# A hybrid decoder block on one core: bias masks moved into the recurrence, indexer loads brought forward, convolution columns moved behind the softmax, softmax division moved to the end

## The chip, the cores and the metric

The kernel runs on one core of a Trainium2 chip. A core has TensorE (PE, matrix products; its weight loads are listed as PEld), VectorE (DVE), ScalarE (ACT), GpSimd (POOL) and SyncE (SP, which here only issues DMAs). Matrix products end in PSUM; everything else works from SBUF, and DMAs move data to and from device memory. The metric is the device time of one execution in microseconds, lower is better.

## What is computed

One layer of a decoder block over 512 tokens of width 1024, all in float32. The part that the change touches:

```
h = adaLN(RMSNorm(x), c)              # c gives shifts, scales and gates ("modulation")
z = h @ w_in                          # columns: attention | RWKV | convolution | 3 gates
o_attn = dsa_attention(z_attn, positions, rel_bias)
o_rwkv = rwkv7_mix(z_rwkv, ...)       # a recurrence over the tokens, 8 heads of 64
o_conv = c_b * causal_dwconv(c_c * c_x)
merged = sum(sigmoid(z_gate_i) * (o_i @ w_branch[i]))
x = x + g1 * (merged @ w_o);  then a ConvGLU feed-forward with its own adaLN; final RMSNorm

# dsa_attention, per query block of 128:
score = sum_h relu(qi_h . ki) * wi_h          # "indexer", 8 heads
keep the 128 best keys of each query
logits = q . k / 8 + rel_bias[bucket(pos_q - pos_k)]    # 32 buckets
o = softmax(logits over the kept keys) @ v
```

## The kernel before

The program is written as a sequence of tile operations. A planner lays it down as one fixed stream per engine: among the instructions whose inputs and buffers it expects to be ready, it takes the one that stands first in the program. `tc.high_priority(offset=n)` moves a block ahead by n places in that ranking (a negative n moves it back), and `tc.issue_after(ins)` keeps a block's instructions behind `ins` on the engine of `ins`. The engines then run their streams in order and wait on semaphores.

**Columns.** `z_col` computes 128 columns of `h @ w_in`, transposed: 8 blocks of 128 rows, three matmuls of 512 columns each (lines 177 to 179), since every float is split into a high and a low part (the split of the weights is at lines 163 on ScalarE and 165 on GpSimd, three buffers each). These column matmuls have no dependence on the attention or the recurrence, so they fill TensorE wherever the chains leave room. The order in the program is: RWKV columns and their chunk preparation; the inversion of a triangular 32x32 system on VectorE (the loop with lines 569 and 571); a DMA round trip for its result (`Dm`); the recurrence in 8 steps (lines 608 to 648); its norm (lines 656 to 675); 12 convolution columns with `conv3`; the attention columns (4 of the indexer's queries, one for its keys and weights, 4 of q, 4 of k, then v); the indexer and top-k; the softmax; then three branches (RWKV, convolution, attention), each with 8 gate columns and 8 branch products.

**Attention columns** are written to device memory as a high and a low part (`split_out`, lines 752 to 755) and loaded again by head: `load_q` and its neighbours issue these loads on GpSimd's queue. The indexer's query and key loads (`qi`, `ki`) stand behind the v columns.

**Bias.** For each key block b, and for 32 groups of 4 keys, VectorE writes a mask tile (line 721: position of the query minus key position at least the threshold of the bucket, 128 rows for 4 keys x 32 buckets, up to 512 queries wide); TensorE multiplies each 128-query block of a mask with the bias differences `dmat` (line 727, two matmuls of 32 columns, high and low part). ScalarE scales the result into `stage` (line 733), and a DMA writes it to `bias_d`. One step is 16 masks; the 8 steps run between the attention columns of q and k. `thr`, the thresholds, come from four loads of the positions early on.

**Indexer and top-k.** 24 pairs of matmuls (`two_pass`, lines 800 and 801), relu on ScalarE, weighted sums on VectorE (832, 834), then 16 rounds of "8 largest" and "replace" for each of three query blocks (839, 840).

**Softmax.** For 4 pairs of heads and 4 query blocks: the bias block is loaded (`bt`), the selection mask is added on GpSimd (867); `two_pass` gives the logits; VectorE adds the bias and takes the row maximum (874) and negates it (876); ScalarE takes the exponential with row sums (878); VectorE takes reciprocals (879) and multiplies each row (881); TensorE transposes the 128x128 blocks (885); ScalarE copies them into `pT` (889). When all four query blocks of a pair are there, 8 matmuls of up to 512 columns give the output, transposed (894), and ScalarE copies it to `o_at` (897).

**Modulation.** `ada_parts` loads 256 KB pieces of `ada_w` and sums them on VectorE (215, 217); one such step is issued with `next(ada)`: four in the k columns, four for each gate column. `finish` ends each group of 8 with TensorE (202) and VectorE (203).

**Memory.** Tiles live in pools that grow from the left or right end of SBUF; a pool opened after another was closed on the same side takes its space, and waits, tile by tile, for its last users. The bias pool `bi` was on the right, where `att` and `ix` (the indexer's operands) come after it. `wk` is a ring of four 512-wide work tiles.

Of the kernel before, what the change touches and what calls it, by code (L numbers as in the profile page):

```python
# [10 lines left out]
F32 = mybir.dt.float32  # L11
# [48 lines left out]
def hybrid_block(ctx, tc, ins, out, consts, dbg=None, stop=99):  # L60
# [286 lines left out]
    def rel_pos(name, shape, aps, pos0, pool, keep=None):  # L347

        pi, lo_i = (T(name + x, shape, I32, pool=pool) for x in "il")
        for dst, ap in aps:  # L350
            SP.dma_start(dst(pi), ap)
        DVE.tensor_scalar(lo_i, pi, 0xFFFF, None, op0=ALU.bitwise_and)
        DVE.tensor_scalar(pi, pi, 16, None, op0=ALU.arith_shift_right)
        rel = T(name, shape, pool=keep or pool)
# [3 lines left out]
        return rel  # L358

    def bias_operands():  # L360
# [7 lines left out]
        thr = rel_pos("thr", [128, 4, 32], [  # L368
            ((lambda t, b=b: t[:, b, :]), dram("positions", b * 128, [[0, 32], [32, 4], [1, 32]])) for b in range(4)], pos0, start.pool, sb)
        DVE.tensor_scalar(thr, thr, kc[:, K_THR:K_THR + 1], None, op0=ALU.add)  # L370
# [25 lines left out]
        return pos0, thr, pw, dmat  # L396

    with tc.issue_after(h_last):
        pos0, thr, pw, dmat = bias_operands()
# [155 lines left out]
    ep.close()  # L555

# [9 lines left out]
    for s_ in range(31):  # L566
# [4 lines left out]
        DVE.tensor_tensor(Ts[:, s_ + 1:, :w], Ts[:, s_ + 1:, :w], t_, op=ALU.add)  # L571
# [28 lines left out]

    S_ = None
    for c in range(8):
        if c:
# [80 lines left out]
    cvp = left_pool("cvp")  # L684
    o_cv = T("o_cv", [128, 4, 512], pool=cvp.pool)

# [6 lines left out]
    for m in range(4):  # L693
        ps_c = z_col(C_CONV + 512 + m * 128)
        cc = wk()
        ACT.activation(cc, ps_c, AF.Copy)
        ps_x = z_col(C_CONV + 1024 + m * 128)
        DVE.tensor_tensor(cc, cc, ps_x, op=ALU.mult)
        cy = wk()
        conv3(cy, cc, cw[:, m, :])  # L700
        ps_b = z_col(C_CONV + m * 128)
        DVE.tensor_tensor(o_cv[:, m, :], cy, ps_b, op=ALU.mult)  # L702
    tap("o_conv", o_cv)


    adp = left_pool("adp")
    bi = right_pool("bi")

    posq = rel_pos("posq", [128, S], [(lambda t: t, dram("positions", 0, [[0, 128], [1, S]]))], pos0, bi.pool)
    bias_d = tc.dram_tile([4, 128, H, 4, 128], F32, name="bias_d")  # L710

    def bias_steps():
        for b in range(4):
            n = S - 128 * b
            stage = {}
            for half in range(2):
                mk = []
                for g in range(16):
                    gg = half * 16 + g
                    m_ = T("mk", [128, 512], F16, tag="mk", bufs=18, pool=bi.pool)  # L720
                    DVE.tensor_scalar(m_[:, :n], posq[:, b * 128:], thr[:, b, gg:gg + 1], None, op0=ALU.is_ge)  # L721
                    mk.append(m_)
                for qb in range(b, 4):
                    ps = sd_bank()
                    for g in range(16):
                        for i in range(2):
                            PE.matmul(ps[:, g * 32:(g + 1) * 32], mk[g][:, (qb - b) * 128:(qb - b + 1) * 128],  # L727
                                      dmat[:, i].rearrange("p j h -> p (j h)"), start=(i == 0), stop=(i == 1))
                    if half == 0:
                        stage[qb] = T("stage", [128, 8, 4, 2, 16], tag="stage", bufs=4, pool=bi.pool)  # L730
                    src = ps.rearrange("p (g j h) -> p h j g", g=16, j=4)
                    for hh in range(2):
                        ACT.activation(stage[qb][:, hh * 4:hh * 4 + 4, :, half, :], src[:, hh * 4:hh * 4 + 4], AF.Copy,
                                       scale=pw[:, 0:1])
                    if half == 1:
                        ACT.dma_start(bias_d[qb, :, :, b, :], stage[qb].rearrange("p h j t g -> p h (j t g)"))
                yield

    bias = bias_steps()


# [15 lines left out]
    def att_cols(c0, slot, scale):  # L757
        for i in range(4):
            if slot == 1:
                next(ada, None)  # L760
            if slot < 2:
                next(bias, None)
            split_out(z_att[slot, i], z_col(c0 + i * 128), scale)

# [5 lines left out]
    ACT.dma_start(z_wi, t[64:72])  # L770
    att_cols(C_ATT, 0, HD ** -0.5)
# [13 lines left out]
    bi.close()  # L785
    op_ = left_pool("op")

    def load_q(dst, z, t0, n):

        row = 2 * 512
        for hh in range(2):
            src = bass.AP(tensor=z.tensor, offset=z.offset + hh * 512 + t0, ap=[[row, 64], [64 * row + (1 - 2 * hh) * 512, 2], [1, n]])
            POOL.dma_start(dst[hh * 64:(hh + 1) * 64], src)
# [6 lines left out]
    att = right_pool("att")  # L803
    vtok = T("vtok", [128, 4, 512], pool=att.pool)
# [521 lines left out]
```

## Time and profile before

| | |
|---|---|
| runs | 1184.8, 1196.58, 1198.01 us; median 1196.58 |
| the profiled execution | 1197.88 us, of which the span (first to last instruction) 1196.2 |
| mean granted TensorE clock | 0.95 |
| TensorE busy | 91% of the span |
| VectorE, ScalarE, GpSimd busy | 64%, 37%, 30% |

The span is read stage by stage: busy time of each engine in a stretch says which of them bounds it, the granted clock says whether TensorE ran at its full 2.4 GHz (1.00) or at 1.2 (0.50), and the waits say what an idle engine was waiting for.

### The profile page before, as it was taken

The page shows a single profiled execution, that of the slowest core. Times are in us where ns is not written, and L with a number is a line of the kernel's source. Part 1 is how long each engine was busy: PE and PEld are TensorE (multiplying, and loading weights), DVE is VectorE, ACT ScalarE, POOL GpSimd, SP SyncE. Part 2 cuts the span into 40 slices and gives each one's busy share as a digit, 9 for nine tenths or more (in the row PEclk, how much of TensorE's full clock was granted, in tenths as well). Part 3 has the DMA queues.
Part 4 walks back from the last instruction along what each step waited for, and adds up shares of the span by engine and source line. Part 5 has one row for each costly group of instructions (what it writes and reads, how often), then busy time and mean ns, then how long its engine had stood idle before and what let it go on. Part 6 is the DMA issues. An engine that isn't in the chain of part 4 may idle for free.

```text
span 1196.2 us, 17528 instructions
## 1 busy us (share of the span) xinstructions
PE 1093.3 (91%) x6710; PEld 877.2 (73%) x6710; DVE 763.9 (64%) x1363; ACT 447.3 (37%) x765; POOL 363.7 (30%) x254
## 2 busy tenths in 40 slices
PE   4889899799999989998887999998899999999996
PEld 3667678577767875876655778877898888888885
DVE  5888777732587828798555454468866766762326
ACT  4243332132334322422333443446543444542213
POOL 3233233322222430565455210003443455200001
PEclk9899899899989975998899999999999999999998
DMA  9641123322336990279766343522233333462201
GB/s 324 183 107 42 39 75 91 88 61 60 115 98 193 302 247 9 76 208 233 211 186 152 91 132 101 176 84 89 75 85 106 87 90 106 141 229 92 97 5 71
DMA packets 191074, 148.26 MB, mean 124 GB/s; under 512 B 18148, under 2 KB 167038, under 8 KB 190990
## 3 DMA queue, kind: packets, MB, share of 16 engines
q1 hardware_dynamic: 162605, 122.57, 35.5%
q10 hardware_dynamic: 23056, 14.53, 4.1%
q0 software_dynamic: 5328, 10.03, 3.8%
q8 instruction: 53, 0.87, 0.3%
q14 instruction: 32, 0.25, 0.1%
HBM read 128.48 MB, written 18.63 MB: 123 GB/s over the span
## 4 chain that ended last, share of the span: by engine, by line
PE 59%; DVE 21%; issue 8%; DMA 7%; ACT 3%; POOL 2%; SPq 0%; ACTq 0%; DVEq 0%; POOLq 0%
PE mm L177 6%; PE mm L179 6%; PE mm L178 6%; DMA xraw<-in_ada_w 3%; PE sd L177 2%; PE sd L178 2%; PE sd L179 2%; PE sd L801 2%; PE sd L1250 2%; PE sd L1252 2%; PE sd L1251 2%; PE sd L1047 2%; DVE acc L217 2%; PE sd L1049 2%; PE sd L1048 2%
## 5 line engine op out<-in xcount | busy, mean ns | idle before, releaser
L165 POOL TENSOR_TENSOR wlo<-wraw,whi 128x1024 fp32r<-128x1024 f32 (+1 forms) x70 | 157.1, 2246 | 279.6 <-ACT whi L163 222.1
L178 PE MATMUL mm<-h_lo,whi 128*128 128x512 f32 (+2 forms) x496 | 203.3, 410 | 1.5 <-DVE h_lo L1076 1.5
L177 PE MATMUL mm<-h_hi,whi 128*128 128x512 f32 (+2 forms) x496 | 203.7, 412 | 0.7 <-DVE o_cv L702 0.7
L179 PE MATMUL mm<-h_hi,wlo 128*128 128x512 f32 (+2 forms) x496 | 203.4, 410 | 0.0
L163 ACT ACTIVATE whi<-wraw 128x1024 fp32r<-128x1024 f32 (+1 forms) x86 | 80.2, 935 | 221.2 <-PE mm L178 95.2
L178 PEld LDWEIGHTS mm<-h_lo,whi 128*128 128x128 f32 (+1 forms) x496 | 96.2, 194 | 24.5 <-issue 3.3
L177 PEld LDWEIGHTS mm<-h_hi,whi 128*128 128x128 f32 (+1 forms) x496 | 96.0, 194 | 23.0 <-issue 4.2
L179 PEld LDWEIGHTS mm<-h_hi,wlo 128*128 128x128 f32 (+1 forms) x496 | 96.3, 194 | 22.1 <-issue 2.4
L1017 DVE TENSOR_TENSOR wlo<-wraw,whi 128x1024 fp32r<-128x1024 f32 x46 | 64.5, 1403 | 58.9 <-ACT whi L1016 58.3
L1016 ACT ACTIVATE whi<-wraw 128x1024 fp32r<-128x1024 f32 x46 | 48.7, 1059 | 75.7 <-PE sd L1252 27.7
L217 DVE SCALAR_TENSOR_TENSOR acc<-xraw,ccol,acc 128x512 f32<-128x512 f32 x56 | 55.7, 994 | 26.1 <-DMA xraw<-in_ada_w 25.7
L1034 POOL TENSOR_TENSOR fS<-wraw 128x512 f32<-128x512 f32 x13 | 19.8, 1526 | 155.3 <-DMA wraw<-in_ffn_w_up 142.5
L1047 PE MATMUL sd<-mg_hi,shi 128*128 128x256 f32 x156 | 45.1, 289 | 7.8 <-DVE p L1190 7.8
L1017 DVE TENSOR_TENSOR slo<-wraw,shi 128x1024 fp32r<-128x1024 f32 x28 | 34.9, 1247 | 21.6 <-ACT shi L1016 21.5
L721 DVE TENSOR_SCALAR mk<-posq,thr 128x512 f16<-128x512 f32 (+3 forms) x128 | 44.7, 424 | 4.1 <-PE sd L727 4.1
L1293 POOL TENSOR_TENSOR f<-f 128x512 f32<-128x512 f32 x4 | 5.7, 1415 | 134.8 <-ACT wk L993 134.8
L177 PE MATMUL sd<-h_hi,whi 128*128 128x512 f32 x112 | 44.5, 397 | 0.0
L1048 PE MATMUL sd<-mg_lo,shi 128*128 128x256 f32 x156 | 44.4, 285 | 0.0
L1049 PE MATMUL sd<-mg_hi,slo 128*128 128x256 f32 x156 | 44.4, 285 | 0.0
L178 PE MATMUL sd<-h_lo,whi 128*128 128x512 f32 x112 | 44.3, 396 | 0.0
L179 PE MATMUL sd<-h_hi,wlo 128*128 128x512 f32 x112 | 44.2, 395 | 0.0
L177 PE MATMUL mm<-o,whi 128*128 128x512 f32 x96 | 39.9, 416 | 3.2 <-DVE modc L203 3.2
(521 smaller groups left out, 2780.7 us busy)
## 6 DMA issues: line engine op xcount, KB each, us to landing
wraw<-in_w_in SPq DMA_DIRECT2D x61, 512.0 KB, 4.3
xraw<-in_ada_w SPq DMA_DIRECT2D x96, 256.0 KB, 4.4
wraw<-in_ffn_w_up SPq DMA_DIRECT2D x44, 512.0 KB, 3.9
wraw<-in_ffn_w_down SPq DMA_DIRECT2D x22, 512.0 KB, 3.4
wraw<-in_w_branch SPq DMA_DIRECT2D x24, 256.0 KB, 3.8
bias_d<-stage ACTq DMA_DIRECT2D x10, 512.0 KB, 5.2
wraw<-in_w_o SPq DMA_DIRECT2D x8, 512.0 KB, 3.8
z_att<-wk ACTq DMA_DIRECT2D x12, 256.0 KB, 2.2
```

Of the source, the lines that this page charges most:

```text
L163: ACT.activation(hi, raw, AF.Copy)
L165: lo_engine[0].tensor_tensor(lo, raw, hi, op=ALU.subtract)
L177: PE.matmul(ps, hi[:, k, :], ahi[:, k0 + k, :], start=start and k == 0, stop=False)
L178: PE.matmul(ps, hi[:, k, :], alo[:, k0 + k, :], start=False, stop=False)
L179: PE.matmul(ps, lo[:, k, :], ahi[:, k0 + k, :], start=False, stop=stop and k == kt - 1)
L217: DVE.scalar_tensor_tensor(acc, raw, ck, acc, op0=ALU.mult, op1=ALU.add)
L721: DVE.tensor_scalar(m_[:, :n], posq[:, b * 128:], thr[:, b, gg:gg + 1], None, op0=ALU.is_ge)
L1016: ACT.activation(hi, src, AF.Copy)
L1017: DVE.tensor_tensor(lo, src, hi, op=ALU.subtract)
L1047: PE.matmul(ps, w[0][:, k], b[0][:, k], start=first and k == 0, stop=False, skip_group_check=True)
L1048: PE.matmul(ps, w[0][:, k], b[1][:, k], start=False, stop=False, skip_group_check=True)
L1049: PE.matmul(ps, w[1][:, k], b[0][:, k], start=False, stop=k == 3, skip_group_check=True)
```

## The change

- The bias pool moves to the left side, is opened before the inversion, and its masks become at most 256 queries wide (17 buffers). A step is 16 masks for one or two query blocks, 12 steps in all; each half of a block is scaled and written to `bias_d` by itself, in runs of 64 keys. The query positions are loaded after the inversion's last instruction, and `thr` is made from them on VectorE instead of from its own loads.
- One bias step stands in each of the 8 recurrence steps and one in each attention column, until there are none left; all of it is ranked 3000 places back and, on VectorE, kept behind the inversion.
- The loads of `qi`, `ki` and `wiT` stand right behind the indexer's columns, all on GpSimd's queue. `att` and `ix` are opened before the attention columns.
- The 12 convolution columns stand behind the softmax, ahead of the branches. The pools of the modulation (`adp`), of the branch operands (`op`) and of the convolution result (`cvp`) are opened behind the bias pool, in its space.
- Modulation steps: none in the k columns, three for each gate column instead of four.
- Softmax: the row operation computes the negated maximum directly; each half's exponential follows it; the transposes take the undivided exponentials; each query block has its own products (128 queries x 64, key block by key block), which one VectorE multiplication divides by the row sums; four transposes at the end of a pair give the layout of `o_at`.

```diff
-    def rel_pos(name, shape, aps, pos0, pool, keep=None):
-        pi, lo_i = (T(name + x, shape, I32, pool=pool) for x in "il")
+    def rel_pos(rel, src):
+        pi, lo_i = (T("wk", [128, 512], I32, tag="wk", bufs=4) for _ in range(2))
+        SP.dma_start(pi, src)
...
-        thr = rel_pos("thr", [128, 4, 32], [
-            ((lambda t, b=b: t[:, b, :]), dram("positions", b * 128, [[0, 32], [32, 4], [1, 32]])) for b in range(4)], pos0, start.pool, sb)
...
+    bi = left_pool("bi")
...
+        sub_last = DVE.tensor_tensor(Ts[:, s_ + 1:, :w], Ts[:, s_ + 1:, :w], t_, op=ALU.add).ins
...
+    posq = T("posq", [128, S], pool=bi.pool)
+    with tc.issue_after(sub_last):
+        rel_pos(posq, dram("positions", 0, [[0, 128], [1, S]]))
+        thr = T("thr", [128, 4, 32])
+        pos4 = posq.rearrange("p (b g j) -> p b g j", b=4, j=4)
+        DVE.tensor_scalar(thr, pos4[:, :, :, 0], kc[:, K_JM:K_JM + 1], None, op0=ALU.mult)
+        for j in range(1, 4):
+            DVE.scalar_tensor_tensor(thr, pos4[:, :, :, j], kc[:, K_JM + j:K_JM + j + 1], thr, op0=ALU.mult, op1=ALU.add)
+        DVE.tensor_scalar(thr, thr, kc[:, K_THR:K_THR + 1], None, op0=ALU.add)
+    def bias_steps():
+        for b in range(4):
+            for qbs in [q for q in ((0, 1), (2, 3)) if q[1] >= b]:
+                qbs = [q for q in qbs if q >= b]
+                n = 128 * len(qbs)
+                for half in range(2):
+                    mk = []
+                    for g in range(16):
+                        gg = half * 16 + g
+                        m_ = T("mk", [128, 256], F16, tag="mk", bufs=17, pool=bi.pool)
+                        DVE.tensor_scalar(m_[:, :n], posq[:, qbs[0] * 128:qbs[0] * 128 + n], thr[:, b, gg:gg + 1], None, op0=ALU.is_ge)
+                        mk.append(m_)
+                    for i, qb in enumerate(qbs):
+                        ps = sd_bank()
+                        for g in range(16):
+                            for d in range(2):
+                                PE.matmul(ps[:, g * 32:(g + 1) * 32], mk[g][:, i * 128:(i + 1) * 128],
+                                          dmat[:, d].rearrange("p j h -> p (j h)"), start=(d == 0), stop=(d == 1))
+                        stage = T("stage", [128, 8, 64], tag="stage", bufs=2, pool=bi.pool)
+                        ACT.activation(stage, ps.rearrange("p (k h) -> p h k", h=8), AF.Copy, scale=pw[:, 0:1])
+                        ACT.dma_start(bias_d[qb, :, :, b, half * 64:half * 64 + 64], stage)
+                    yield
+    def bias_step():
+        with tc.high_priority(offset=-3000), tc.issue_after(sub_last):
+            next(bias, None)
     S_ = None
     for c in range(8):
+        bias_step()
...
+    att = right_pool("att")
+    ix = right_pool("ix")
...
     def att_cols(c0, slot, scale):
         for i in range(4):
-            if slot == 1:
-                next(ada, None)
-            if slot < 2:
-                next(bias, None)
+            bias_step()
             split_out(z_att[slot, i], z_col(c0 + i * 128), scale)
...
     ACT.dma_start(z_wi, t[64:72])
+    for i in range(4):
+        load_q(qi[:, i], z_att[2, i], 128, 384)
+    for hh in range(2):
+        POOL.dma_start(ki[hh * 64:(hh + 1) * 64], z_ki)
+    POOL.dma_start(wiT, z_wi)
     att_cols(C_ATT, 0, HD ** -0.5)
...
-                DVE.tensor_tensor_reduce(lg[hh][:, :n], ps[:, :n], bt[:, hh, :n], 1.0, -3.0e38, op0=ALU.add, op1=ALU.max,
+                DVE.tensor_tensor_reduce(lg[hh][:, :n], ps[:, :n], bt[:, hh, :n], -1.0, 3.0e38, op0=ALU.add, op1=ALU.min,
                                          accum_out=rs[:, 0, hh:hh + 1])
-            DVE.tensor_scalar(rs[:, 1], rs[:, 0], -1.0, None, op0=ALU.mult)
+                ACT.activation(lg[hh][:, :n], lg[hh][:, :n], AF.Exp, bias=rs[:, 0, hh:hh + 1], scale=-1.0,
+                               accum_out=rs[:, 1, hh:hh + 1])
+            DVE.reciprocal(rs[:, 2], rs[:, 1])
+            po = sd_bank()
             for hh in range(2):
-                DVE.tensor_scalar(lg[hh][:, :n], lg[hh][:, :n], rs[:, 0, hh:hh + 1], None, op0=ALU.mult)
                 pt = sd_bank()
                 for b in range(qb + 1):
+                    PE.transpose(pt[:, b * 128:(b + 1) * 128], lg[hh][:, b * 128:(b + 1) * 128], ident)
+                pT = M("pT", [128, 512])
+                ACT.activation(pT[:, :n], pt[:, :n], AF.Copy)
+                h = 2 * pr + hh
+                for b in range(qb + 1):
+                    PE.matmul(po[:, hh * 64:(hh + 1) * 64], pT[:, b * 128:(b + 1) * 128], vtok[:, b, h * 64:(h + 1) * 64],
+                              start=(b == 0), stop=(b == qb))
+            DVE.tensor_tensor(o_tok[:, qb].rearrange("p (h d) -> p h d", h=2), po[:, :128].rearrange("p (h d) -> p h d", h=2),
+                              rs[:, 2].unsqueeze(2).to_broadcast([128, 2, 64]), op=ALU.mult)
         po = sd_bank()
...
+        for qb in range(4):
+            PE.transpose(po[:, qb * 128:(qb + 1) * 128], o_tok[:, qb], ident)
         ACT.activation(o_at[:, pr, :], po, AF.Copy)
...
-                for _ in range(4):
+                for _ in range(3):
                     next(ada, None)
```

## Rows read from the trace of the kernel before

**Rows 1.** Page, busy time of each engine: us, share of the span, instructions.
```profile
PE 1093.3 (91%) x6710; PEld 877.2 (73%) x6710; DVE 763.9 (64%) x1363; ACT 447.3 (37%) x765; POOL 363.7 (30%) x254
```

**Rows 2.** Windows: length, busy us (instructions) of PE PEld DVE ACT POOL, clock, DMA share, GB/s.
```profile
228.20:255.00 26.80, 19.73 (x308) 15.61 (x308) 9.11 (x14) 9.36 (x13) 11.21 (x5) 0.81 0.45 104
255.00:310.00 55.00, 54.51 (x572) 42.35 (x572) 18.16 (x36) 15.86 (x33) 12.27 (x10) 1.00 0.18 51
...
346.40:408.50 62.10, 61.81 (x799) 45.99 (x800) 54.75 (x142) 25.24 (x52) 16.37 (x6) 0.95 0.69 206
...
438.80:476.00 37.20, 37.20 (x77) 19.55 (x76) 27.18 (x79) 11.62 (x23) 5.30 (x5) 0.54 0.18 57
...
564.40:702.70 138.30, 121.52 (x519) 85.62 (x519) 77.68 (x177) 51.44 (x125) 54.71 (x41) 0.94 0.59 153
702.70:760.00 57.30, 57.30 (x249) 46.43 (x249) 27.08 (x36) 21.45 (x31) 2.95 (x4) 1.00 0.47 129
```

**Rows 3.** Windows around the slices of lower clock, same columns.
```profile
344.20:346.40 2.20, 0.13 (x1) 0.00 (x0) 2.20 (x3) 0.00 (x0) 1.53 (x1) 0.99 0.43 163
346.40:353.20 6.80, 6.74 (x80) 4.54 (x80) 6.80 (x18) 0.00 (x0) 0.00 (x0) 0.50 0.40 116
421.40:426.50 5.10, 0.43 (x3) 0.21 (x2) 0.75 (x1) 2.49 (x3) 2.42 (x2) 0.84 1.35 287
424.90:431.70 6.80, 5.22 (x24) 5.22 (x25) 0.00 (x0) 0.53 (x2) 4.92 (x4) 0.50 1.23 324
441.90:476.00 34.10, 34.10 (x64) 17.56 (x63) 25.58 (x77) 9.46 (x18) 2.20 (x4) 0.50 0.18 54
578.50:585.30 6.80, 6.80 (x18) 5.09 (x18) 1.81 (x8) 1.10 (x4) 2.67 (x3) 0.50 1.26 298
```

**Rows 4.** Waits of TensorE, 564 to 703 us: total us, times, longest.
```profile
PE sd L885 <- DVE lg L881: 16.7, 10, 3.7
```

**Rows 5.** Waits of all engines, 340 to 705 us, same columns.
```profile
PEld sd L894 <- ACT pT L889: 2.2, 7, 0.4
```

**Rows 6.** Timeline of one softmax step: start us, us, instruction [idle before <-releaser].
```profile
596.35 0.08 DVE L874 DVE_READ_ACCUMULATOR2_ANT rs<- 128x1 f32 x1
...
602.02 0.75 DVE L217 SCALAR_TENSOR_TENSOR acc<-xraw,ccol,acc 128x512 f32<-128x512 f32 x1 [3.11 <-DMA xraw<-in_ada_w]
602.69 0.16 DVE L879 RECIPROCAL rs<-rs 128x2 f32<-128x2 f32 x1
...
603.42 1.12 PE L885 MATMUL sd<-ident,lg 128*128 128x128 f32 x8 [2.43 <-DVE lg L881]
```

**Rows 7.** Timelines of TensorE, three places, same columns.
```profile
272.64 1.67 PE L625 MATMUL sd<-UV,HYL 128*128 128x64 f32 x14
...
388.22 1.76 PE L727 MATMUL sd<-dmat,mk 128*128 128x32 f16 x64
...
604.77 2.85 PE L894 MATMUL sd<-pT,vtok 128*64 128x512 f32 x16
```

**Rows 8.** Masks on VectorE, two shapes, then all: count, busy us, mean ns, idle before.
```profile
L721 DVE TENSOR_SCALAR mk<-posq,thr 128x128 f16<-128x128 f32 x32 | 10.4, 393 | 0.0
L721 DVE TENSOR_SCALAR mk<-posq,thr 128x256 f16<-128x256 f32 x32 | 9.8, 381 | 1.6 <-PE sd L727 1.6
...
L721 DVE TENSOR_SCALAR mk<-posq,thr 128x512 f16<-128x512 f32 (+3 forms) x128 | 44.7, 424 | 4.1 <-PE sd L727 4.1
```

**Rows 9.** The masks' tile (ns minimum/median/maximum), then a timeline from 190 us.
```profile
L721 DVE TENSOR_SCALAR mk<-posq,thr x128: 270/407/2483, 345.9 to 401.6; 128x512 f16<-128x512 f32 x32, 128x384 f16<-128x384 f32 x32, 128x256 f16<-128x256 f32 x32, 128x128 f16<-128x128 f32 x32
...
192.71 2.43 POOL L165 TENSOR_TENSOR wlo<-wraw,whi 128x1024 fp32r<-128x1024 f32 x1 [3.14 <-ACT whi L163]
192.92 2.31 DVE L571 TENSOR_TENSOR sub<-sub,st 128x60 f32<-128x60 f32 x1
```

**Rows 10.** Groups of GpSimd, 255 to 310 us: count, busy us, mean ns, idle before.
```profile
L165 POOL TENSOR_TENSOR wlo<-wraw,whi 128x1024 fp32r<-128x1024 f32 (+1 forms) x4 | 8.5, 2136 | 16.6 <-PE mm L179 9.4 <-ACT whi L163 7.3
L632 POOL TENSOR_TENSOR Sp<-S,pc 128x256 f32<-128x256 f32 x6 | 3.7, 621 | 25.6 <-DVE S L636 17.3 <-DVE S L638 8.4
```

**Rows 11.** Groups of VectorE, 564.4 to 702.7 us, same columns.
```profile
L881 DVE TENSOR_SCALAR lg<-lg,rs 128x128 f32<-128x128 f32 (+3 forms) x32 | 16.9, 569 | 0.5
```

More of the change, by code (lines that the diff above doesn't have):

```diff
@@ L691, in conv3 @@
         DVE.scalar_tensor_tensor(dst[:, 2:], src[:, :510], wts[:, 0:1], dst[:, 2:], op0=ALU.mult, op1=ALU.add)
[L693 to L739, printed above, removed]
+    att = right_pool("att")
+    ix = right_pool("ix")
     z_att = tc.dram_tile([3, 4, 128, 2, 512], F32, name="z_att")
@@ L770, in hybrid_block @@
     ACT.dma_start(z_wi, t[64:72])
+    vtok = T("vtok", [128, 4, 512], pool=att.pool)
+    sel = {0: cmask}
+    for qb in range(1, 4):
+        sel[qb] = T("sc", [128, (qb + 1) * 128], tag="sc%d" % qb, pool=att.pool)
+    qi = T("qi", [128, 4, 2, 384], F32R, pool=ix.pool)
+    for i in range(4):
+        load_q(qi[:, i], z_att[2, i], 128, 384)
+    ki = T("ki", [128, 2, 512], F32R, pool=ix.pool)
+    for hh in range(2):
+        POOL.dma_start(ki[hh * 64:(hh + 1) * 64], z_ki)
+    wiT = T("wiT", [8, 512], pool=ix.pool)
+    POOL.dma_start(wiT, z_wi)
     att_cols(C_ATT, 0, HD ** -0.5)
@@ L785, in hybrid_block @@
     bi.close()
+    adp = left_pool("adp")
     op_ = left_pool("op")
[L791 to L796, printed above, removed]
+    cvp = left_pool("cvp")
+    o_cv = T("o_cv", [128, 4, 512], pool=cvp.pool)
     def two_pass(ps, q, hh, q0, k_hi, k_lo, n):
@@ L877, in hybrid_block @@
+            DVE.reciprocal(rs[:, 2], rs[:, 1])
+            po = sd_bank()
             for hh in range(2):
-                ACT.activation(lg[hh][:, :n], lg[hh][:, :n], AF.Exp, bias=rs[:, 1, hh:hh + 1], accum_out=rs[:, 2, hh:hh + 1])
-            DVE.reciprocal(rs[:, 0], rs[:, 2])
-            for hh in range(2):
-                DVE.tensor_scalar(lg[hh][:, :n], lg[hh][:, :n], rs[:, 0, hh:hh + 1], None, op0=ALU.mult)
                 pt = sd_bank()
                 for b in range(qb + 1):
-                    j = (b, qb - b)[hh]
-                    PE.transpose(pt[:, j * 128:(j + 1) * 128], lg[hh][:, b * 128:(b + 1) * 128], ident)
-                flat = pT.rearrange("p r q -> p (r q)")
-                o, step = ((qb + 1) * 128, 640) if hh == 0 else ((3 - qb) * 640, 768)
-                dst = bass.AP(tensor=flat.tensor, offset=flat.offset + o, ap=[list(flat.ap[0]), [step, qb + 1], [1, 128]])
-                ACT.activation(dst, pt[:, :n].rearrange("p (b q) -> p b q", q=128), AF.Copy)
@@ L890, in hybrid_block @@
-        po = sd_bank()
-        for b in range(4):
-            for hh in range(2):
-                h = 2 * pr + hh
-                PE.matmul(po[hh * 64:(hh + 1) * 64, b * 128:], vtok[:, b, h * 64:(h + 1) * 64],
-                          pT[:, b, (b + 1) * 128:] if hh == 0 else pT[:, 3 - b, :(4 - b) * 128],
-                          start=(b == 0), stop=(b == 3), skip_group_check=True)
+                    PE.transpose(pt[:, b * 128:(b + 1) * 128], lg[hh][:, b * 128:(b + 1) * 128], ident)
+                pT = M("pT", [128, 512])
@@ L945, in split_o @@
         return o
+    for m in range(4):
+        ps_c = z_col(C_CONV + 512 + m * 128)
+        cc = wk()
+        ACT.activation(cc, ps_c, AF.Copy)
+        ps_x = z_col(C_CONV + 1024 + m * 128)
+        DVE.tensor_tensor(cc, cc, ps_x, op=ALU.mult)
+        cy = wk()
+        conv3(cy, cc, cw[:, m, :])
+        ps_b = z_col(C_CONV + m * 128)
+        DVE.tensor_tensor(o_cv[:, m, :], cy, ps_b, op=ALU.mult)
+    tap("o_conv", o_cv)
     branch(1, split_o(o_rw), True, False)
@@ L952, in hybrid_block @@
     mg.close()
+    cvp.close()
     op_.close()
     adp.close()
-    cvp.close()
     mid.close()
```

34 lines of the change are left out of this document (9 added, 25 removed).

## The prediction

> **What bounds the kernel now.** I read the busy shares first. TensorE is busy 91% of the span and VectorE 64% [rows 1], so TensorE is the bound on average, and a part pays only where it shortens TensorE's own stream: its work, its idle time, or the time at the lower clock. Where those lie is read from the windows by stage [rows 2]. The change touches what stands between the triangular inversion (about 184 us) and the end of the merge (760 us). The last stage, 702.7 to 760, is the measure of a good stretch: TensorE busy all of it at full clock, 249 matmuls in 57.3 us, 0.23 us for each 512-wide one. Against that, the softmax (564.4 to 702.7) leaves TensorE 16.8 us idle at a mean clock of 0.94. The indexer (438.8 to 476) has no idle time but a mean clock of 0.54. The bias stage (346.4 to 408.5) is full on TensorE and 54.8 of 62.1 us on VectorE. The recurrence (255 to 310) is full on TensorE and only 18.2 of 55 on VectorE: there is room for masks.
>
> Next come the waits of TensorE inside the softmax: 16.7 of its idle microseconds, in ten waits, are transposes waiting for line 881, the division on VectorE [rows 4]. One step shows why [rows 6]: the row maxima are done at 596.43, but the reciprocal starts at 602.69 behind a piece of the modulation sum that itself waits for its load, and the transposes start at 603.42. The lower clock comes in short slices [rows 3]: in each the granted clock is 0.50, that is 1.2 instead of 2.4 GHz, mostly just behind an idle stretch (344.2 to 346.4, then 346.4 to 353.2).
>
> **Late division and the per-block product.** It removes from each of 16 steps two multiplications and a negation on VectorE (16.9 us in all for the multiplications [rows 11]) and, what counts, puts no VectorE instruction between exponential and transpose. In the step shown the transposes could start some 5 us sooner. TensorE's 16.7 us of waits are taken to go. With them go the slices at half clock in this stage: 6.8 us as shown, and two of 3.4 more like it [rows 3]; half of 13.6 is 6.8 us. Bounds: if only the two latest operations go and the order of the queues brings waits back, about half of the 23.5 stays; below nothing I see none, since an edge is removed.
>
> It adds TensorE work. Before, a pair of heads is 8 plain-float matmuls (16 records in 2.85 us, [rows 7]). After, it is 20 products of 64 columns, two records each, 40 records. The nearest row is the state update of the recurrence, the same 128x128 stationary and 64 moving columns: 14 records in 1.67 us, 0.119 each. So 40 x 0.119 = 4.76, plus four transposes at 1.12 / 8 = 0.14 each [rows 6], 0.56. That is 5.3 against 2.85, **+2.5 us a pair, +9.9 in all**, and it lies on the path because TensorE is the bound. The 16 scalings of 128 elements on VectorE are free beside the instructions they replace.
>
> The change also adds a wait: each half's products stand right behind the copy of its transposed block (line 889's work), 32 times. Behind a product that waits on TensorE stand gate and convolution columns that were ready. Before, such waits were 7, 2.2 us in all, 0.31 each [rows 5]. Bounds 0 (the second half's transposes cover the first copy) to 32 x 0.31 = 10; I take **+5**, the first half covered, the second not.
>
> **Bias steps moved ahead.** The 640 products are the same. 64 of them take 1.76 us [rows 7], so 17.6 us of TensorE before and after. Masks: before, 32 of each width from 512 to 128; after, 128 of 256 and 64 of 128 columns, at 0.31 and 0.33 us [rows 8]: 39 + 21 = 60 against 44.7 us. That is 15 us more on VectorE, costing nothing while it hides in the recurrence's 36.8 idle us and the wait for the inverse before it (228.2 to 255: VectorE 9.1 of 26.8). What is gained: the place at 344.2 where TensorE waited for the first masks, 2.1 us idle, and the half-clock slice behind it, 6.8 / 2 = 3.4 us [rows 3]: **-5.5**. The 20 stores instead of 10 stand on ScalarE's queue; ScalarE is busy a third of the time, and DMA has 0.18 to 0.45 of its share in these stages [rows 2]: nothing. One strided evacuation of 512 elements for two of 256: nothing.
>
> **Masks beside GpSimd.** The longest mask took 2483 ns, the median 407; and a 60-element sum on VectorE that began at 192.92 took 2.31 us, ending just after a subtraction on GpSimd from 192.71 to 195.14 [rows 9]. So a VectorE instruction issued beside a GpSimd one can be held for its whole length. The Trainium skill, "SBUF — State Buffer", section "Who interferes with whom", says the same and speaks against this edit: VectorE's `tensor_scalar` forms and two-input forms and GpSimd take a shared port pair as an exclusive lock, and the second one blocks fully. By that rule a mask put between two links of the recurrence can hold the next link; what it would give here is rival D.
>
> **Indexer loads as soon as possible.** Eight loads of `qi`, two of `ki` and now `wiT` are issued on GpSimd right behind the indexer's columns, not behind the values. Before, TensorE idled 4.7 of the 5.1 us from 421.4, and the slice behind it ran at half clock, 5.2 busy us of it, 2.6 lost [rows 3]: 7.3 us. The issues do not vanish; they move ahead of weight subtractions elsewhere on the same GpSimd queue, and `qi` lies in space that the recurrence frees, so GpSimd may wait there with weights queued behind it. Bounds 0 to 7.3; I take half, **-3.6**.
>
> **Columns.** The 12 convolution columns (288 matmuls) leave the place before the attention columns, so the attention columns fill the inversion, the recurrence and the norm, and the indexer can begin some 66 us (288 x 0.23) sooner. That is no gain by itself: the same matmuls stand later, as filling of top-k and softmax. The stall at 228 (TensorE 19.7 of 26.8) stays, since the DMA round trip behind the inversion is unchanged. Three modulation steps a gate instead of four, none in the key columns, and its pool now in the masks' space: the same loads later, still before the residual; nothing. The threshold built from the broadcast positions instead of four loads: nothing.
>
> **Sum**, on the profiled execution's 1197.9 (span 1196.2; the median of the runs is 1196.6, lowest 1184.8): -16.7 -6.8 +9.9 +5 -5.5 -3.6 = -17.7, giving **1180**.
>
> **Rivals.**
> A, the indexer too. 34.1 us of it run at half clock [rows 3]. It begins with indexer matmuls alone; with masks' products and convolution columns about, the clock may stay up. At most half, 17; I take 10 more: 1170. Against it: the same matmuls in the same order feed the same scores. Chance 0.12.
> B, the waits change their name. TensorE's stream is laid down beforehand, and the exponential and the copy wait on ScalarE, behind weight roundings. If half of the 23.5 us stays and the copies cost their full 10: 1180 + 11.7 + 5 = 1197, no change. For it: the waits moved from one engine to another in line; against: the chain is shorter by two queue entries. Chance 0.13.
> D, the masks hold the recurrence. GpSimd has four weight subtractions of 2136 ns and six state scalings of 621 ns there, 8.5 + 3.7 = 12.2 us [rows 10]. If each holds one mask and with it one link: 1180 + 12 = 1192. For it: TensorE's stream has a link of this chain every microsecond or two. Against it: only 17 mask buffers, so they fill before the recurrence and stop unless products run. Chance 0.10.
> C, slower: **the masks come last.** The steps have the lowest rank, 3000 instructions behind, and TensorE is full in the recurrence, so their products may get no place until the query, key, value and convolution columns are used up. Then 175 masks remain (192 less 17 buffers), 175 x 0.31 = 54 us of VectorE. The first branch's operand `o` lies in the masks' space and cannot start, so TensorE has the products, 17.6, and four gate columns (the four `wk` buffers), 4 x 24 x 0.23 = 22: 40 us. It idles 14 us, or 36 if the gates were done too; the middle, 25, and a half-clock slice of 3.4: 1180 + 28 = 1208. It decides once more than 40 / 0.31 = 129 masks are left when the columns end. For it: TensorE has no idle time in 255 to 310. Against it: top-k leaves gaps in which masks can be made while convolution columns last. Chance 0.22.
>
> **How the numbers follow.** The forecast has 0.43, its own range 1170 to 1191 from the halves of the terms above. A measurement of this kernel tells about 1% from no change (one of three runs of before lies 1% under the others), so faster means below 1184.6 and slower above 1208.5. Faster: two thirds of the forecast's 0.43, nearly all of A, a little of B to D: 0.43. Slower: half of C, and the upper ends of B and D: 0.17. Same: 0.40. The range leaves out a tenth at either end, the lower half of A and the upper part of C: 1164 to 1212.
>
> **What would show it.** Right: in the softmax, transposes wait for the exponential, not for a VectorE result, under 8 us in all; products per pair near 5 us; masks between 235 and 310; no idle time at 344. Wrong: VectorE busy with masks and TensorE idle once the convolution columns end (C); steps of the recurrence more than the present 55 / 8 = 6.9 us apart, with masks of 2 us between (D); ten or more microseconds of waits for the copy or the exponential (B); the indexer's stretch at a clock above 0.8 (A). The prediction fails altogether if the attention columns do not fill the recurrence, for then TensorE idles there and nothing above applies.

## The result and the profile after

The change made the kernel slower: 1257.45 us median (1255.11 to 1265.11) against 1197.3 for the kernel before, **ratio 1.0533 [1.0444, 1.0622]**. The forecast was 1180, in a range of 1164 to 1212. One thing about the reference: executions of the kernel before fall into two groups, 1174 to 1192 us at a granted clock near 0.96 and 1195 to 1207 near 0.947; three of the four behind 1.0533 and the one whose rows stand ahead of the prediction (clock 0.950) are of the second, the ratios of the experiments go by the first alone, and by its one run here, 1184.8, the changed kernel stands at 1.06. The experiments are therefore compared with the changed kernel by their medians, and stages by their rows.

The page of the changed kernel, busy times, against [rows 1]:

```profile
PE 1110.9 (88%) x6822; PEld 911.2 (73%) x6822; DVE 752.2 (60%) x1394; ACT 443.8 (35%) x745; POOL 363.9 (29%) x255
```

TensorE's busy time grew by 18 us (the softmax's new products and transposes alone take 13.5 more, rows of e6 and e10 below); its share fell to 88%. The rest of the loss is idle time and clock. From 160 us to the end of the merge, windows of the kernel before, then of the changed kernel (columns as in [rows 2]):

```profile
160.00:759.90 599.90, 556.38 (x3626) 419.97 (x3627) 379.59 (x759) 199.51 (x370) 199.19 (x132) 0.93 0.51 136
```

```profile
160.00:815.40 655.40, 571.97 (x3731) 451.71 (x3730) 367.55 (x787) 196.56 (x348) 199.79 (x133) 0.87 0.47 125
```

55.5 us more in all: TensorE idles 83.4 instead of 43.5 us, and the mean clock is 0.87 instead of 0.93. Everything behind the merge is within 5 us. By stage, the changed kernel:

```profile
195.40:216.20 20.80, 0.02 (x1) 0.00 (x0) 19.29 (x48) 1.42 (x2) 2.34 (x1) 0.61 0.12 37
250.00:355.00 105.00, 104.28 (x566) 88.03 (x565) 13.97 (x16) 28.90 (x37) 43.72 (x19) 1.00 0.49 140
355.00:426.00 71.00, 62.38 (x865) 54.98 (x864) 48.43 (x146) 19.20 (x37) 11.53 (x8) 0.73 0.29 66
426.00:441.00 15.00, 0.10 (x2) 0.00 (x0) 11.43 (x16) 2.67 (x3) 4.35 (x8) 0.50 0.26 48
...
488.00:518.00 30.00, 30.00 (x88) 15.65 (x87) 23.67 (x79) 11.08 (x24) 0.70 (x2) 0.51 0.28 72
600.00:711.00 111.00, 99.21 (x492) 76.29 (x492) 54.35 (x126) 47.11 (x119) 57.44 (x44) 0.90 0.60 158
711.00:815.40 104.40, 104.40 (x473) 85.35 (x472) 63.19 (x83) 32.80 (x48) 12.59 (x9) 1.00 0.57 168
```

Read the second line first. The recurrence had run at 255 to 310 [rows 2]; here, from 250 until just before 355, TensorE does little but columns, and VectorE is busy 14 of 105 us. The recurrence comes afterwards, with few columns left: a granted clock of 0.73, then 15 us in which TensorE waits for the norm. TensorE's waits from 160 to 816 us name these holes and the 20.8 us at 195:

```profile
PE mm L177 <- DVE wk L743: 20.8, 1, 20.8
PE sd L707 <- DVE MV L701: 14.9, 1, 14.9
PE mm L178 <- DVE o L929: 9.6, 1, 9.6
PE sd L870 <- ACT lg L863: 9.5, 3, 5.9
```

The second recurrence step has no wait of its own; a timeline of TensorE shows it simply standing behind the columns (L624 are bias products, L646 the step's first product, whose state had been ready since 251):

```profile
353.97 0.40 PE L179 MATMUL mm<-h_hi,wlo 128*128 128x512 f32 x1
354.21 0.81 PE L624 MATMUL sd<-dmat,mk 128*128 128x32 f16 x26
354.95 0.68 PE L646 MATMUL sd<-S,AR 64*64 64x64 f32 x16
```

So the planner put it there. A ring is a fixed number of buffers that a group of tiles uses in turn. The planner's order can be read from the built program: for each tile of a ring, in the order of the program, the place in the planner's order at which it is first and last used.

```
ring sd (5 banks)                              first  last
sd_1762  bias, first step, second bank          1714  2876
sd_1809  recurrence c = 0, ph                   1884  1921
sd_1855  bias, second step, first bank          2663  2896
sd_1891  bias, second step, second bank         2713  3001
sd_1927  recurrence c = 1, px                   2714  2735

ring wk (4 buffers)
wk_1679  positions, pi (loaded by SP)            440  1478
wk_1680  positions, lo_i                        1465  1475
wk_3058  first attention column, high part      1466  1476
```

Between 1921 and 2663 four of five sd banks are free, yet `px` gets one only in the place right behind the bias step's second. In wk, `pi` alone holds a buffer just before place 1465, yet the first column gets one only in the place behind `lo_i`, whose first writer (line 351) is held behind the last link of the inversion (place 1464). **Theory 1**: a ring is handed out in the order of the program. A low-ranked or held-up user that stands early shuts it for all later users, whatever their rank. Rivals: the columns moved behind the softmax are missing (2); the early loads hold GpSimd (3); the low rank does harm by itself (4).

### The profile page after: what moved, and what is told of

Read it like the earlier page. It is cut to its first block, busy times and chain, and to the rows that moved or that the text cites. A ratio compares the mean times of both kernels' runs of the same rounds, so it can differ in the third digit from the quotient of the medians.

```text
span 1256.3 us, 17710 instructions
## 1 busy us (share of the span) xinstructions
PE 1110.9 (88%) x6822; PEld 911.2 (73%) x6822; DVE 752.2 (60%) x1394; ACT 443.8 (35%) x745; POOL 363.9 (29%) x255
## 4 chain that ended last, share of the span: by engine, by line
PE 36%; DVE 6%; DMA 3%; ACT 2%; issue 2%; POOL 1%; POOLq 0%; DVEq 0%; ACTq 0%; SPq 0%
PE mm L178 4%; PE mm L179 4%; PE mm L177 4%; DMA wraw<-in_ffn_w_up 2%; PE sd L177 2%; PE sd L178 2%; PE sd L179 2%; PE sd L1247 2%; PE sd L1249 2%; PE sd L1248 2%; DVE wlo L1014 1%; PE sd L875 1%; PE sd L1044 1%; PE mm L1248 1%; PE mm L1249 1%
## 5 line engine op out<-in xcount | busy, mean ns | idle before, releaser
L177 PE MATMUL mm<-h_hi,whi 128*128 128x512 f32 (+2 forms) x496 | 200.6, 406 | 22.6 <-DVE wk L743 20.8
L178 PE MATMUL mm<-h_lo,whi 128*128 128x512 f32 (+2 forms) x496 | 198.8, 401 | 1.6 <-DVE h_lo L1073 1.5
L179 PE MATMUL mm<-h_hi,wlo 128*128 128x512 f32 (+2 forms) x496 | 198.6, 401 | 1.2 <-POOL wlo L165 1.2
L217 DVE SCALAR_TENSOR_TENSOR acc<-xraw,ccol,acc 128x512 f32<-128x512 f32 x56 | 60.7, 1084 | 23.4 <-DMA xraw<-in_ada_w 22.7
L618 DVE TENSOR_SCALAR mk<-posq,thr 128x256 f16<-128x256 f32 (+1 forms) x192 | 58.7, 373 | 11.4 <-PE sd L624 11.2
L178 PE MATMUL mm<-o,whi 128*128 128x512 f32 x96 | 40.8, 425 | 9.6 <-DVE o L929 9.6
L177 PE MATMUL mm<-o,whi 128*128 128x512 f32 x96 | 40.5, 424 | 8.0 <-DVE modc L203 7.0
```

Source lines behind the costliest of these rows:

```text
L177: PE.matmul(ps, hi[:, k, :], ahi[:, k0 + k, :], start=start and k == 0, stop=False)
L178: PE.matmul(ps, hi[:, k, :], alo[:, k0 + k, :], start=False, stop=False)
L179: PE.matmul(ps, lo[:, k, :], ahi[:, k0 + k, :], start=False, stop=stop and k == kt - 1)
L217: DVE.scalar_tensor_tensor(acc, raw, ck, acc, op0=ALU.mult, op1=ALU.add)
L618: DVE.tensor_scalar(m_[:, :n], posq[:, qbs[0] * 128:qbs[0] * 128 + n], thr[:, b, gg:gg + 1], None, op0=ALU.is_ge)
```

## Experiments

All ratios are to the kernel before in the same job. "Second step" is the start of the first product that reads the state, line 646 of the changed kernel: 261.2 us before and 355.0 after. These products in the kernel before, the changed one, e2, e3 and e4 (nanoseconds minimum/median/maximum, first and last start in us; the line number shifts with the edits):

```profile
L608 PE MATMUL sd<-S,AR x112: 218/218/267, 261.2 to 303.9; 64*64 64x64 f32 x112
L646 PE MATMUL sd<-S,AR x112: 218/311/366, 355.0 to 418.8; 64*64 64x64 f32 x112
L646 PE MATMUL sd<-S,AR x112: 218/218/267, 250.8 to 304.8; 64*64 64x64 f32 x112
L645 PE MATMUL sd<-S,AR x112: 218/218/267, 250.1 to 292.8; 64*64 64x64 f32 x112
L646 PE MATMUL sd<-S,AR x112: 218/311/367, 252.3 to 304.2; 64*64 64x64 f32 x112
```

**e1, late division alone.** The kernel before with the changed softmax part.

> The kernel before with the softmax inner part of the changed kernel alone (late division, products per block, four transposes a pair); bias stage, columns and loads stay as they were. Theory 1 (the loss of the change comes from the recurrence that is held back, the softmax part is a gain): the waits of the transposes on VectorE's division, 16.7 us before, fall under 8 us, TensorE's busy time in the softmax stage grows by about 10 us, the stage ends 8 to 25 us earlier, and the time is 1172 to 1190 us. Theory 2 (the softmax stage of the changed kernel is shorter only because the convolution columns fill it; the division as such buys nothing): 1190 to 1205 us.

Measured: 1189.55 us, 1.0047 [1.0006, 1.0089]. No gain; the time is at the upper edge of theory 1's range, but the kernel before took 1189.2 beside it, so theory 2 of this run came nearer. TensorE's waits on the division are gone, and this stands in their place (waits of TensorE, 160 us to the end):

```profile
PE sd L883 <- ACT lg L876: 10.0, 4, 4.7
```

**e2, rank in place.**

```diff
-        with tc.high_priority(offset=-3000), tc.issue_after(sub_last):
+        with tc.issue_after(sub_last):
```

> The changed kernel, with the bias steps at the rank of their place instead of 3000 places later; nothing else differs. Theory 1 (the planner gives out the five sd banks in the order of the program, so a bias step that stands ahead of a recurrence step but ranks behind the columns keeps the bank queue shut, and the recurrence with it): the second recurrence step starts within 15 us of the first one's end, about 255 us instead of 355, the recurrence is over by 330 us, the half-clock stretch at 391 to 446 us goes, and the time is 1175 to 1215 us. Theory 2 (the columns moved behind the softmax are what is missing; order does not matter): 1235 to 1260 us, with TensorE idle elsewhere. Theory 3 (the early indexer loads hold GpSimd, and with it the Sp of the recurrence): the second step still starts later than 300 us, time over 1230 us.

Measured: 1206.5 us, 1.0161 [1.0109, 1.0213]; second step at 250.8, recurrence over by 307. By medians 51 us come back (from 1257.45) by one line that only ranks. Theories 2 and 3, as causes of the held recurrence, are out: columns and loads are unchanged. The wait at 195 remains (waits of TensorE in e2, 160 to 830 us):

```profile
PE mm L177 <- DVE wk L743: 20.8, 1, 20.8
```

**e3, about the same rank, later place.**

```diff
-        bias_step()              # in the recurrence's loop
-        with tc.high_priority(offset=-3000), ...
+        with tc.high_priority(offset=-2000), ...
```

> The changed kernel without the bias steps in the recurrence: all twelve stand in the attention columns, 2000 places behind their own, which is about the rank that the first eight had. Theory 1 (bank queue): no bias bank stands ahead of the recurrence, so the second step starts at about 250 us and the recurrence is over by 320 us although rank and columns are as in the changed kernel; the bias products come in one run after the columns, for some 40 to 60 us with few columns beside them and part of it at the half clock; time 1195 to 1235 us. Theory 4 (the low rank alone does the harm, wherever the steps stand): 1245 to 1265 us. Theory 3 (indexer loads): the second step starts after 300 us.

Measured: 1246.5 us, 1.0495 [1.0451, 1.0538]. The second step starts at 250.1, as theory 1 says; but the time is above theory 1's range and inside theory 4's. Both hold: the low rank also puts the products late by itself, here behind the convolution columns (the first of them starts at 433.7), and what follows is bare (windows of e3: columns, bias, indexer):

```profile
317.00:434.00 117.00, 115.93 (x700) 96.00 (x701) 24.95 (x27) 31.20 (x39) 48.93 (x29) 1.00 0.48 124
434.00:484.00 50.00, 47.81 (x653) 33.17 (x649) 46.61 (x182) 16.30 (x27) 2.34 (x1) 0.55 0.50 112
484.00:530.00 46.00, 39.45 (x87) 21.81 (x86) 36.77 (x109) 13.90 (x26) 4.21 (x4) 0.65 0.16 41
```

**e4, the same place and rank, another ring.** The bias products take their banks from mm, the columns' ring.

```diff
-                        ps = sd_bank()
+                        ps = mm_bank()
```

> The changed kernel with the bias products in the three banks of the columns (mm) instead of the five of the small products (sd); place and rank of the steps are the same. Theory 1 (bank queue of the tag): the recurrence is no longer held, its second step starts by 265 us; the columns are now the ones that queue behind the bias steps, so the recurrence runs with bias products between its steps and few columns; time 1190 to 1235 us. Theory 4 (rank): the second step still starts after 340 us and the time stays at 1245 to 1265 us. Theory 3 (indexer loads): as theory 4.

Measured: 1232.5 us, 1.0352 [1.0288, 1.0417]; second step at 252.3. Place and rank are as in the changed kernel, only the ring differs, and the recurrence is free. Now the columns are shut out instead: TensorE stands still from 189 until the first masks exist, behind a bias product that holds the first place in mm's row (timeline of TensorE):

```profile
222.09 2.07 PE L624 MATMUL mm<-dmat,mk 128*128 128x32 f16 x30 [32.91 <-DVE mk L618]
```

The sd ring and the mm ring thus each show theory 1, though the hold of the wk ring, 195 to 216 us in the changed kernel, falls into the same hole. The time is in theory 1's range.

**e5, positions off the wk ring** (rank as changed).

```diff
-        pi, lo_i = (T("wk", ..., tag="wk", bufs=4) for _ in range(2))
+        pi, lo_i = (T("stage", ..., tag="stage", bufs=2, pool=bi.pool) for _ in range(2))
```

> The changed kernel, with the two buffers of the position arithmetic taken from the stage ring (free until the first bias bank is copied) instead of the wk ring; nothing else differs. Theory 1 (a ring is given out in the order of the program): in the changed kernel the second of these buffers is first written by VectorE behind the whole inversion, and every later user of wk, the attention columns' parts above all, is handed its buffer only after it; that is the idle time of 20.8 us at 195 to 216. Without it the columns' low parts run between the inversion's steps, TensorE idles under 3 us in there, and the time falls by 14 to 30 us to 1225 to 1243. Rival (VectorE has no room between the steps of the inversion, so the low parts come late in any case): the idle time stays over 12 us and the time is 1247 to 1262 us.

Measured: 1245.9 us, 1.0523 [1.0465, 1.0581]. The idle time is gone (window of e5):

```profile
187.00:215.00 28.00, 28.00 (x136) 21.61 (x136) 20.47 (x40) 8.92 (x13) 11.28 (x7) 1.00 0.57 173
```

VectorE had room between the inversion's steps, so the rival is out, but the time lies above theory 1's range too: by medians only 11.5 us of the forecast 14 to 30 come back. The run of columns ends 10 us sooner and the second step, still held, comes at 345.4. The rest of the gain shows once the recurrence is free (e6).

**e6, both repairs** (e2 and e5).

> Both repairs: bias steps at the rank of their place, position arithmetic off the wk ring; everything else is the changed kernel. If the two held-up rings are the whole loss: the 1206 us of the first repair less 15 to 25, that is 1180 to 1192 us, level with the kernel before. If the columns moved behind the softmax or the early loads cost something by themselves: 1195 to 1210 us.

Measured: 1181.3 us, 0.9994 [0.9960, 1.0028]. The whole loss is gone: 76 us by medians, 25 of them after e2. That the time is near the forecast 1180 is luck: by the ratio this kernel gains nothing on the one before. The window from 160 us to the merge's end in e6:

```profile
160.00:744.30 584.30, 548.45 (x3757) 434.64 (x3754) 381.98 (x796) 212.72 (x362) 195.72 (x134) 0.95 0.52 141
```

Idle time 35.9 instead of 83.4 us, clock 0.95 instead of 0.87. The next runs take this kernel as their base.

**e7, bias steps with the columns**, none in the recurrence, rank of their place.

> Both repairs, and all twelve bias steps in the attention columns at the rank of their place, none in the recurrence. If the masks in the recurrence are the better place (VectorE is free there): slower than with the steps in the recurrence by 5 to 15 us, because the masks then bound TensorE after the recurrence, at the half clock: 1190 to 1207 us. If they disturb the recurrence more than they help: 1172 to 1185 us.

Measured: 1201.1 us, 1.0163 [1.0106, 1.0220]: the recurrence is the better place, by 1.7% and more than expected. Outside it VectorE has no air (window of e7 over the bias stage, against 54.75 of 62.1 in [rows 2]):

```profile
345.00:401.00 56.00, 55.46 (x785) 41.45 (x784) 54.25 (x178) 17.44 (x26) 16.45 (x5) 1.00 0.57 144
```

**e8, convolution columns ahead of the indexer** in the program.

> Both repairs, and the convolution columns back ahead of the indexer and the softmax in the program (behind the attention columns). If columns are needed more in the indexer and at the start of branch 1 than behind the softmax: fewer than 5 us of idle TensorE between 390 and 450 instead of about 12, and 8 to 15 us faster than with the columns behind. If it only moves them: within 6 us of it.

Measured: 1191.2 us, 1.0067 [1.0030, 1.0105]: neither expectation; behind the softmax is better by about 0.7%. TensorE's idle time between 390 and 450 us did go, as the first expectation had it, but waits for the exponential came back, and the profiled clock was 0.941 against 0.956. The window in e8 and in e6, and the wait in e8 (160 to 765 us; e6 has none):

```profile
390.00:450.00 60.00, 60.00 (x256) 47.14 (x254) 36.34 (x38) 17.07 (x24) 26.41 (x11) 1.00 0.58 178
390.00:450.00 60.00, 47.07 (x170) 32.23 (x171) 57.70 (x148) 17.96 (x30) 14.19 (x9) 0.89 0.23 67
PE sd L882 <- ACT lg L875: 9.5, 3, 4.4
```

**e9, the recurrence's branch ahead of the convolution columns.**

> Both repairs, and the convolution columns behind the recurrence's branch instead of ahead of it; nothing else differs. With both repairs TensorE idles 12.9 us at 430 waiting for a convolution product that VectorE runs behind the indexer's selection, in a stretch (390 to 450 us) in which VectorE is busy 57.7 of 60 us. The columns of the recurrence's branch are read by ScalarE and GpSimd. If that wait is what is left: it goes, and the time is 8 to 15 us under the 1181 us of the kernel with both repairs. If VectorE's parts of the adaptive weights or of the split stall the columns of the branch in the same way: no change, within 5 us of it.

Measured: 1189.3 us, 0.9963 [0.9926, 1.0000]: no clear change by the ratio (e6: 0.9994), 8 us slower by the medians of e6 and of e11 (below), which ran in this job; not the gain hoped for by either. The 12.9 us went; in their place, among TensorE's waits of e9:

```profile
PE mm L202 <- DVE acc L217: 10.1, 1, 10.1
```

**e10, early division** in the repaired kernel.

> Both repairs, with the softmax inner part of the kernel before (division ahead of the transposes); the rest is the changed kernel. By the prediction's terms the late division is worth 16.7 + 6.8 less 14.9, so this kernel would be 8.6 us slower than with it, 1185 to 1195 us. By the first run (late division alone in the kernel before: no measurable difference) it is within 5 us of it, 1176 to 1186 us. If the extra products and transposes only cost, now that columns fill the softmax at the full clock: 5 to 12 us faster.

Measured: 1208.0 us, 1.0166 [1.0134, 1.0198]: 1.7% slower than with the late division by the ratios, 26.6 us or 2.3% by the median of e11 in the same job, whose other difference, the place of the loads, is worth nothing (e13, e14). Either is over twice the 8.6 us of the prediction's terms. TensorE's waits, 160 to 765 us:

```profile
PE sd L872 <- DVE lg L868: 24.1, 13, 7.9
```

**e11, loads late**, in the repaired kernel.

> Both repairs, with the indexer's loads back behind the v columns in the program; the rest is the changed kernel. By the prediction's term the early loads are worth 3.6 us: 1182 to 1188 us. If they are hidden anyway or cost nothing: within 3 us of the kernel with both repairs, 1178 to 1185 us. If GpSimd is better off without them among the low parts: faster by 3 us or more.

Measured: 1181.4 us, 0.9877 [0.9826, 0.9928]. By its median it is e6; by its ratio, faster. The kernel before had moved between the two jobs, so both were run side by side.

**e13 and e14, e6's and e11's kernels side by side.**

> The kernel with both repairs once more (loads early, as changed), for the comparison with e14 on the same chip and the same runs of the kernel before. If early loads cost what the two jobs seemed to show: 10 to 14 us slower than e14. If the jobs differed: within 4 us of e14.

> The kernel with both repairs and the indexer's loads behind the v columns once more. If the loads' place matters: 10 to 14 us faster than e13 and about 0.988 of the kernel before. If the jobs differed: within 4 us of e13, and 0.988 to 1.0 of the kernel before. By the prediction's term it would be 3.6 us slower than e13.

Measured: e13 1182.2 us, 0.9972 [0.9933, 1.0012]; e14 1181.0 us, 0.9976 [0.9932, 1.0019]. The early loads are worth nothing either way, and e11's 0.9877 was its job.

**e12, no VectorE readers beside the selection.**

```diff
-                for _ in range(3):
+                for _ in range(0 if first else 5):
                     next(ada, None)
```

(and the branch first as in e9, the loads late as in e11)

> Both repairs, indexer loads late, the recurrence's branch ahead of the convolution columns, and the steps of the adaptive weights out of that branch (five instead of three at each gate of the other two, the total stays covered). In the stretch of the indexer's selection the columns then have readers on ScalarE and GpSimd alone. If the waits of 12.9 us (convolution product) and 10.1 us (adaptive weights) are what is left there: both go, idle TensorE between 390 and 450 us is under 5 us, and the time is 6 to 13 us under that of e14 beside it. If VectorE, 57 of 60 us busy, holds the columns by a third way (the split of the branch's input): within 4 us of e14.

Measured, in one job with e14: 1169.4 us, **0.9869 [0.9805, 0.9932]**, six runs; 11.5 us under e14 by medians. The stretch of the selection, e14 and then e12:

```profile
390.00:450.00 60.00, 47.08 (x178) 33.40 (x177) 58.01 (x148) 16.17 (x25) 15.29 (x8) 0.89 0.21 55
```

```profile
390.00:450.00 60.00, 57.30 (x231) 42.56 (x232) 57.37 (x130) 22.19 (x36) 32.68 (x20) 1.00 0.33 93
```

VectorE is as full as before; TensorE idles 2.7 us instead of 12.9, and the clock stays up: the first expectation. This version lies under both kernels. After e11, I would hold only its sign, not the second digit, for settled.

## Why the prediction was wrong

**The step that failed** is "Bias steps moved ahead": that the masks hide in the recurrence and cost nothing there. It asked whether VectorE had room (it had) and not whether the recurrence would still run where it did. It was put off by 94 us, because a bias step 3000 places behind stood ahead of it in the sd ring, and the masks did not hide in it: only 28 of the 192 were made before 353 us. The closing sentence, that all fails if the attention columns do not fill the recurrence, looked at the wrong side: the columns ran, and the recurrence was missing. e2, e3 and e4 part place, rank and ring as causes of the held recurrence. They do not split the time between them: e3 frees the recurrence and is still only 11 us faster, since it keeps the low rank and stands in the place that costs e7 20 us against e6.

**Second, "the threshold built from the broadcast positions instead of four loads: nothing."** The wait on the inversion's end (`sub_last`) was written in the diff, and the two temporaries sat in wk, which every column needs: 20.8 us idle. I asked who is queued behind a waiting instruction on its engine, and not who is queued behind its buffer.

By medians the repairs together take 1257.45 to 1181.3; e2 alone to 1206.5, e5 alone to 1245.9. The merge's end in the profiles: 815.4 as changed, 807.5 in e5, 761.5 in e2, 744.3 in e6.

**Rival C** was right in its first half: TensorE was full of columns, and only 54 of the 640 products got a place before 354. From 353 us on, 164 masks were still to be made (C counts 175; line of the changed kernel, 353 to 520 us):

```profile
L618 DVE TENSOR_SCALAR mk<-posq,thr x164: 270/339/2562, 356.0 to 494.0; 128x256 f16<-128x256 f32 x100, 128x128 f16<-128x128 f32 x64
```

Its 28 us are too low because it lets the recurrence run in time: here the recurrence and its norm, with the 15 us hole, stood behind these bias steps too. e3 shows C as it was written, 50 us of bias nearly without columns at a granted clock of 0.55. **Rival A** did not happen: the indexer's stretch, 488 to 518, has a clock of 0.51.

**Late division** was sized -8.6 net. In the repaired kernel it is worth 1.7 to 2.3%, 20 to 27 us (e10 against e6 and e11); alone in the kernel before, nothing (e1). So the terms do not add up, and what in the repaired kernel takes up its gain, for e6 is level with the kernel before, no run isolates. Its terms: 24.1 us of waits in e10 are 0 in e6, but 10.0 for the exponential remain in e1 and 9.5 in the changed kernel, over the 8 that I allowed and, in e1, rival B's sign. TensorE's busy time for the products and new transposes, e6, then the old products, e10 (groups of TensorE, 480 to 720 us):

```profile
L875 PE MATMUL sd<-vtok,pT 128*128 128x64 f32 x160 | 22.4, 271 | 0.0
L881 PE MATMUL sd<-ident,o_tok 128*128 128x128 f32 x16 | 3.1, 272 | 0.0
```

```profile
L881 PE MATMUL sd<-pT,vtok 128*64 128x512 f32 (+3 forms) x64 | 12.0, 499 | 0.0
```

13.5 more, for a forecast 9.9. The +5 for the copies was too dear: no product waited (0.0). The exponential is waited for in e1 and not in e6. The place of the convolution columns bears on that: e8, which differs from e6 only in having them earlier in the program, waits 9.5 us again, and e1 has them early too. By which way, and why the changed kernel waits as long with their place as in e6, is open.

**Masks** took 58.7 us after and 60.8 in e6, for a forecast 60. **Rival D** was right in its mechanism and too dear; the trace agrees with the rule cited there (the Trainium skill, "SBUF — State Buffer", "Who interferes with whom"). In e6 six masks beside a weight subtraction took 4.20 us and held a link of the recurrence (all engines, timeline):

```profile
271.04 4.20 DVE L618 TENSOR_SCALAR mk<-posq,thr 128x256 f16<-128x256 f32 x6
271.94 2.37 POOL L165 TENSOR_TENSOR wlo<-wraw,whi 128x1024 fp32r<-128x1024 f32 x1
275.27 0.42 DVE L648 TENSOR_TENSOR Xs<-sd,MV 128x256 f32<-128x256 f32 x1
```

TensorE waited for such a link twice, 2.1 us each, not 12.2 in all; the steps stand 10.2 us apart (first products of the first and the last at 251.6 and 322.7) instead of 6.9, now with bias products between them. **Loads**, -3.6: nothing (e13, e14). **Columns**, "no gain by itself": behind the softmax is worth about 0.7% (e8). **Bias idle** at 344: gone, as said.

## What to carry to other kernels

Before moving low-ranked work ahead in a planned program, list the rings it draws from (banks, shared temporaries) and who draws later from the same ring: rank and waits pass on to them all, even with buffers free. Leave such work the rank of its place (e2), or give it a ring used only by work that comes after it anyway (e5, e6); a ring of its own was not tried. Where one engine is saturated for a stretch, fill the other one there with work whose results that engine does not read (e12, settled in its sign only).

## Not expected of the hardware

The same program is granted different mean clocks from one execution to the next: the kernel before between 0.939 and 0.967 in one job. A stage's clock in one profiled execution is no fixed term either: the 34.1 us at half clock in [rows 3], on which rival A rested, have no counterpart in e1, whose indexer is the same; its window:

```profile
438.80:476.00 37.20, 37.20 (x137) 23.96 (x137) 34.28 (x103) 15.79 (x29) 12.62 (x10) 1.00 0.30 87
```
